# Starting places of the combinations and their weights in a Strassen-like MLP

## The chip, the cores and the metric

The kernel runs on one core of one Trainium2 chip. The metric is the device time of one execution in microseconds (us). The kernel before takes 1051.84 us (median of 3 runs, 1051.46 to 1052.83). A core has TensorE (matrix multiplication; a load of 128x128 weights and a matmul that streams a moving operand past them are two instructions, PEld and PE in the profile), VectorE (DVE), ScalarE (ACT), GpSimd (POOL) and the DMA queues that SyncE (SP) and POOL fill. SBUF is the working memory of 128 partitions, and a place in it is a byte address within a partition. PSUM takes TensorE's results.

## The reference

A decoder trunk of two layers over 512 tokens of width 1024, in float32. Layer 0 mixes by multi-head latent attention, layer 1 by gated linear attention; each mixer is followed by an MLP.

```python
x = x + mix
x = x + sq_relu_mlp(rms_norm(x, norm_mlp[i]), mlp_w_up[i], mlp_w_down[i])

def sq_relu_mlp(xn, w_up, w_down):          # 1024 -> 4096 -> 1024
    hid = jnp.square(jax.nn.relu(xn @ w_up))
    return hid @ w_down
```

The change lies in the two MLPs alone.

## The kernel before

**Precision.** Every float32 operand is split into a high part (rounded to the type float32r) and a low part (what is left). A product is three matmuls: high weights by high input, high by low, low by high. Weights come from HBM by DMA into `wraw` (1024 columns of 4 bytes per partition) or `comb`; `piece` then takes a buffer `wh` and a buffer `wl` and calls `split`: ACT rounds into `wh` (L104), DVE subtracts into `wl` (L107). Each of the two tags has four buffers of 1152 float32r elements, used in turn by the up products, the down products, and the mixers. The piece's 1024 elements lie at an offset within the 1152: 128 elements as a rule, 120 elements for the up products of the MLPs (`W_AT` and `W_AT_UP`). All these buffers begin 32 bytes past a multiple of 128, so a piece begins 32 + 512 bytes (32 past a multiple of 128) as a rule, and 32 + 480 (at a multiple of 128) for the up products.

**The MLP.** `mlp` cuts the hidden width of 4096 into eight blocks of 512. The first block's up product is made plainly (`up_first`). For the other seven, the up product is made by a scheme with seven products of half-sized blocks in place of eight, the down products likewise. `step` holds one block's sequence: seven `up_product`s for the next block and seven `down_product`s for this one, interleaved in an order written out by hand (`order`, `ends`). Four of the seven up products of a step have as input a linear combination of the input's quadrants, T1 to T4; three have a quadrant itself (`"11"`, `"21"`, `"22"`), which lies in the `set` tiles that the norm has written (hi and lo parts of 512 tokens, 32 bytes past a multiple of 128).

**The combinations.** `quadrants` runs once per MLP, before the first step. DVE and ACT make the four sums in the `comb` buffers 2 to 5 (L882 to L886), and `signed` splits each into a tile of its own, T2, T3, T1, T4: ACT writes the high parts (L837), DVE the low parts (L838). A tile holds 4 blocks of 128 features, each with 256 high and 256 low elements, 8192 bytes per partition. Ahead of the four tiles an unused tile of 120 elements, `gap`, sets their place: it begins 64 bytes past a multiple of 128, so the T tiles begin 32 past one. The pool that holds all this (`fast`) goes over room that the mixer has left; buffers `comb` 0 and 1 are taken after the T tiles.

**An up product** (L949) is 24 matmuls: two blocks of 128 hidden features, four blocks of 128 input features, three parts. Each loads 128x128 weights (512 bytes per partition from `wh` or `wl`) and streams 256 tokens (1024 bytes per partition from `set` or T). In the profile's names the T tiles appear as `T`, the quadrants as `set`:

```python
for n, (a_, x_) in enumerate(((wh, xh), (wh, xl), (wl, xh))):
    PE.matmul(o, a_, x_, ...)
```

**A down product** (L958) is 12 matmuls that load 128x128 of the hidden values and stream 512 columns of `wh` or `wl`.

The order of instructions on each engine is made by a list scheduler from the program's order and a cost model; waits follow from what each instruction reads and writes. While TensorE works at one product, ACT and DVE split the weights of the next ones, SP's queue loads raw weights, and POOL's queue adds second weight quadrants onto them (L928, L938).

Of the kernel before, what the change touches and what calls it, by code (L numbers as in the profile page):

```python
# [10 lines left out]
F32 = mybir.dt.float32  # L11
F32R = mybir.dt.float32r
# [6 lines left out]
P = 128  # L19
# [6 lines left out]
TH = S // 2  # L26
# [24 lines left out]
def trunk_kernel(ctx: ExitStack, tc: tile.TileContext, t_in: dict, out: bass.AP):  # L51
# [7 lines left out]
    def uname(s):  # L59
        count[0] += 1  # L60
        return f"{s}_{count[0]}"
# [40 lines left out]
    def split(src, hi, lo, hi_eng=ACT, lo_eng=DVE, order=lambda i: i):  # L102
        if hi_eng is ACT:
            order(ACT.activation(hi, src, AF.Copy))  # L104
        else:
            hi_eng.tensor_copy(hi, src)
        lo_eng.tensor_tensor(lo, src, f(hi), ALU.subtract)  # L107
# [26 lines left out]
        SP.dma_start(raw, src)  # L134
        return raw

    W_ROOM, W_AT, W_AT_UP = 1152, 128, 120

    def room_for(tag, a, n, at=W_AT):
        t = sb.tile([P, W_ROOM], F32R, tag=tag, bufs=4, name=uname(tag))  # L140
        return t[:, at : at + a * n].rearrange("p (a n) -> p a n", a=a)

    def piece(raw, a, n, order=lambda i: i, at=W_AT):
        hi = room_for("wh", a, n, at)
        lo = room_for("wl", a, n, at)
        split(raw, hi, lo, order=order)
        return hi, lo

    def cut(pair, *idx):
        return tuple(t[idx] for t in pair)  # L150
# [56 lines left out]
    def gcol(name, j):  # L207
        c = GAIN_COL[name] + j
        return gains[:, c : c + 1]
# [170 lines left out]
    def mla(layer, nrm, first, pools):  # L380
# [39 lines left out]
        for h in range(2):  # L420
            ks = slice(h * KH, (h + 1) * KH)
            SP.dma_start(raw[:, ks], w_in[:, :256].rearrange("(k p) n -> p k n", p=P)[:, ks])
            wq.append(piece(raw[:, ks], KH, 256))
# [12 lines left out]

        raw = col_chunk(w_in, 256, P)
        w = piece(raw, ND, P)
        p = bank("b")
        a_type(p, w, X)  # L440
# [33 lines left out]
        for k in range(2):  # L474
            SP.dma_start(raw[:, k], w_ukv[:, k, :, NOPE:])
        wv = [piece(raw[:, k : k + 1].rearrange("p a h c -> p a (h c)"), 1, D) for k in range(2)]
        V = [[None, None] for _ in range(NT)]
        VP = []
# [329 lines left out]
    def mlp(layer, nrm, nxt=None):  # L808
# [3 lines left out]
        KH = ND // 2  # L812
        first, second = slice(0, TH), slice(TH, S)
        es = ExitStack()
        fast = es.enter_context(tc.tile_pool(name=f"fast{layer}", bufs=1, reuse_waits="tile"))
# [11 lines left out]
        def comb(i):  # L827
            return fast.tile([P, 2 * S], F32, tag=f"comb{i}", bufs=1, name=uname("comb"))

        def by_k(t, n):  # L830
            return t.rearrange("p (k n) -> p k n", k=n)
# [4 lines left out]
        def signed(src, hi, lo, sign):  # L836
            ACT.activation(hi, src, AF.Copy, scale=sign)  # L837
            DVE.scalar_tensor_tensor(lo, src, sign, f(hi), ALU.mult, ALU.subtract)  # L838
# [34 lines left out]
        def quadrants():  # L873
            lead, trail = range(KH), range(KH, ND)
            quad["11"] = [nrm.parts[k][:, :, first] for k in lead]
            quad["21"] = [nrm.parts[k][:, :, first] for k in trail]
            quad["22"] = [nrm.parts[k][:, :, second] for k in trail]
            t1, t2, t3, t4 = (by_k(comb(i), KH) for i in range(2, 6))
            for k in lead:
                g1, g2 = (gcol(nrm.g, nrm.g0 + j) for j in (k, k + KH))  # L880
                u, v = xT[k], xT[k + KH]
                ACT.activation(t3[:, k], u[:, second], AF.Copy, scale=g1)  # L882
                DVE.scalar_tensor_tensor(t3[:, k], v[:, second], g2, t3[:, k], ALU.mult, ALU.subtract)
                DVE.scalar_tensor_tensor(t2[:, k], u[:, first], g1, t3[:, k], ALU.mult, ALU.add)
                DVE.scalar_tensor_tensor(t4[:, k], v[:, first], g2, t2[:, k], ALU.mult, ALU.subtract)
                DVE.scalar_tensor_tensor(t1[:, k], v[:, second], g2, t2[:, k], ALU.mult, ALU.subtract)  # L886
            fast.tile([P, 120], F32, tag="gap", name=uname("gap"))
            for name, t, sign in (("T2", t2, -1.0), ("T3", t3, 1.0), ("T1", t1, -1.0), ("T4", t4, -1.0)):
                parts = fast.tile([P, KH, 2, TH], F32R, tag=name, name=uname(name))
                signed(t, parts[:, :, 0], parts[:, :, 1], sign)  # L890
                quad[name] = [parts[:, k] for k in lead]

# [46 lines left out]
            return first_part  # L939

        def up_product(t, a, q, start):
            w = piece(a, KH, 256, at=W_AT_UP)
            for j in range(2):
                o = t[:, j * TH : (j + 1) * TH]
                for k in range(KH):
                    wh, wl = cut(w, slice(None), k, slice(j * P, (j + 1) * P))
                    xh, xl = quad[q][k][:, 0], quad[q][k][:, 1]
                    for n, (a_, x_) in enumerate(((wh, xh), (wh, xl), (wl, xh))):
                        PE.matmul(o, a_, x_, start=start and j == 0 and k == 0 and n == 0, stop=k == KH - 1 and n == 2, skip_group_check=True)  # L949
# [11 lines left out]
        def step(b, q, r, after):  # L961
# [24 lines left out]

            z = bank("u")
            up_product(z, a11, "11", True)
            y = bank("u")
            ACT.activation(y, z, AF.Copy)  # L990
# [5 lines left out]
            e = two_banks("e") if opening else begun(d)  # L996

            up_product(y, a12, "21", False)
            finish(y, 0, 0, r)
            DVE.tensor_tensor(a11, s1, a11, ALU.add)  # L1000
# [15 lines left out]
            def up_t2():  # L1016
                up_product(z, a11, "T2", False)
                u = part["u"] = tmp()
                ACT.activation(u, z, AF.Copy)
                DVE.tensor_tensor(a12, a11, a12, ALU.add)  # L1020
# [57 lines left out]

        up_first(Q[0])
        quadrants()  # L1080
        if not nxt:
            residual()
# [57 lines left out]
        q = Q[(NB - 1) % 2]  # L1140
        if nxt:
            room = [parts_room[(turn[0] + k) % 4] for k in range(4)]
# [5 lines left out]
            for c in range(2):  # L1148
# [10 lines left out]
                for j, p in enumerate(ps_):  # L1159
                    if j % 2 == 0:  # L1160
                        w = piece(last_raw[c][:, :, j * P : (j + 2) * P], 4, 256)
                    for k in range(4):
                        wh, wl = cut(w, slice(None), k, slice(j % 2 * P, (j % 2 + 1) * P))
# [525 lines left out]
    for k0, k1 in ((0, 1), (1, 2), (2, 4), (4, 6), (6, 8)):  # L1689
        w = piece(raw0[:, k0:k1], k1 - k0, KL, tc.keep_in_program_order)  # L1690
# [59 lines left out]
def build(nc, shapes):  # L1750
    args = {}
    for name, (shape, dt) in shapes.items():
        args[name] = nc.dram_tensor(f"in_{name}_dram", shape, dt, kind="ExternalInput").ap()
    o = nc.dram_tensor("out_0_dram", (S, D), F32, kind="ExternalOutput").ap()
    with tile.TileContext(nc) as tc:
        trunk_kernel(tc, args, o)
# [22 lines left out]
```

## Time and profile before

| | |
|---|---|
| median of 3 runs | 1051.84 us (1051.46 to 1052.83) |
| profiled execution | 1052.17 us, its span 1050.4 us |
| TensorE matmuls | 1040.9 us busy (99%), 5966 of them |
| TensorE weight loads | 909.7 us (87%) |
| VectorE, ScalarE, GpSimd | 874.3 us (83%), 699.3 us (67%), 113.9 us (11%) |
| L949, up products | 2352 matmuls: 1344 on T, 1008 on `set` |
| L958, down products | 1176 matmuls |

Matmuls overlap, so the mean duration of one is longer than the distance from start to start; where TensorE never idles, that distance, a step, is what the time is made of. A row of the chain or of the timeline with a count (x48) gives it as length divided by count. In the timeline a row of several gives the time from the first start to the last end. The two MLPs' steps run from about 206 to 476 us and from 747 to 1020 us of the span.

### The profile page before, as it was taken

Reading aid. Unit: us, or ns where it says so; the run is one execution under the profiler, and the core shown is the slowest. Engines: PE = TensorE matmul, PEld = TensorE weight load, DVE = VectorE, ACT = ScalarE, POOL = GpSimd, SP = SyncE. Lnnn points to the kernel's source line nnn. Section 1 sums busy time; section 2 is a strip of 40 time slices with the busy share of each in tenths; the row PEclk is TensorE's granted clock in tenths of the full one; section 3 lists DMA queues with packets and bytes.
Section 4 is the critical chain, followed back from the end, with each engine's and each line's share of the span. In section 5 each row is a group of like instructions: output and inputs, shape, how many; then the busy total and the mean of one; then the engine's idle time right before and its main releaser. Section 6 shows DMA issues by size and latency. Waiting matters only on the chain.

```text
span 1050.4 us, 15641 instructions
## 1 busy us (share of the span) xinstructions
PE 1040.9 (99%) x5966; PEld 909.7 (87%) x5966; DVE 874.3 (83%) x1340; ACT 699.3 (67%) x1074; POOL 113.9 (11%) x128
## 2 busy tenths in 40 slices
PE   9999999999999999999999999999999999999997
PEld 7788888899999999998888888888888999999995
DVE  7889977979889889888687399469889989989993
ACT  7667654677767777776445566555667777777784
POOL 7400010301011011000000000000010101111000
PEclk9999999999999999999999999999999999999999
DMA  7401235776876787843212222165496697687612
GB/s 232 121 21 41 81 96 145 230 194 153 225 201 155 190 221 163 194 160 121 68 64 80 87 75 75 48 162 159 89 249 160 164 240 178 153 232 187 155 61 81
DMA packets 120492, 149.97 MB, mean 143 GB/s; under 512 B 9344, under 2 KB 86144, under 8 KB 120288
## 3 DMA queue, kind: packets, MB, share of 16 engines
q1 hardware_dynamic: 95920, 117.76, 35.2%
q0 software_dynamic: 22400, 29.36, 17.4%
q10 hardware_dynamic: 2096, 1.84, 0.6%
q8 instruction: 47, 0.77, 0.3%
q14 instruction: 29, 0.24, 0.1%
HBM read 144.49 MB, written 4.19 MB: 142 GB/s over the span
## 4 chain that ended last, share of the span: by engine, by line
PE 93%; ACT 3%; DVE 2%; DMA 1%; issue 0%; ACTq 0%; SPq 0%; DVEq 0%
PE ps L949 26%; PE ps L958 26%; PE ps L112 10%; PE ps L114 10%; PE ps L113 10%; PE ps L1165 2%; PE ps L1420 1%; PE ps L129 1%; PE ps L1200 1%; PE ps L414 1%; PE ps L1547 1%; DVE wl L107 1%; PE ps L1470 0%; PE ps L677 0%; ACT wh L104 0%
## 5 line engine op out<-in xcount | busy, mean ns | idle before, releaser
L958 PE MATMUL ps<-wh,set 128*128 128x512 f32 x784 | 252.9, 391 | 0.1
L104 ACT ACTIVATE wh<-wraw 128x1024 fp32r<-128x1024 f32 x139 | 146.6, 1058 | 98.4 <-PE ps L113 39.4
L107 DVE TENSOR_TENSOR wl<-wraw,wh 128x1024 fp32r<-128x1024 f32 x139 | 169.7, 1221 | 46.1 <-ACT wh L104 45.2
L958 PEld LDWEIGHTS ps<-wh,set 128*128 128x128 f32 x784 | 147.0, 188 | 29.8 <-ACT set L104 0.5
L949 PE MATMUL ps<-T,wh 128*128 128x256 f32 x896 | 159.2, 279 | 0.0
L958 PE MATMUL ps<-wl,set 128*128 128x512 f32 x392 | 153.2, 391 | 0.0
L107 DVE TENSOR_TENSOR wl<-comb,wh 128x1024 fp32r<-128x1024 f32 x112 | 136.3, 1217 | 17.8 <-ACT wh L104 17.8
L949 PEld LDWEIGHTS ps<-T,wh 128*128 128x128 f32 x896 | 138.7, 188 | 2.7
L104 ACT ACTIVATE wh<-comb 128x1024 fp32r<-128x1024 f32 x112 | 118.0, 1054 | 25.5 <-PE ps L949 10.0
L949 PE MATMUL ps<-T,wl 128*128 128x256 f32 x448 | 125.0, 279 | 0.0
L949 PE MATMUL ps<-set,wh 128*128 128x256 f32 x672 | 119.7, 279 | 0.0
L112 PE MATMUL ps<-set,wh 128*128 128x512 f32 x280 | 109.5, 391 | 0.0
L113 PE MATMUL ps<-set,wh 128*128 128x512 f32 x280 | 109.4, 391 | 0.0
L114 PE MATMUL ps<-set,wl 128*128 128x512 f32 x280 | 109.1, 390 | 0.0
L949 PEld LDWEIGHTS ps<-set,wh 128*128 128x128 f32 x672 | 104.5, 188 | 2.6
L949 PE MATMUL ps<-set,wl 128*128 128x256 f32 x336 | 93.8, 279 | 0.0
L958 PEld LDWEIGHTS ps<-wl,set 128*128 128x128 f32 x392 | 73.6, 188 | 13.0
L949 PEld LDWEIGHTS ps<-T,wl 128*128 128x128 f32 x448 | 84.2, 188 | 0.1
L938 POOL DMA_DIRECT2D comb<-in_mlp_w_down_dram x28 | 33.8, 1207 | 302.0 <-DMA comb<-in_mlp_w_down_dram 112.8
L949 PEld LDWEIGHTS ps<-set,wl 128*128 128x128 f32 x336 | 63.2, 188 | 0.0
L113 PEld LDWEIGHTS ps<-set,wh 128*128 128x128 f32 x280 | 52.6, 188 | 10.8 <-DVE set L743 0.2
L114 PEld LDWEIGHTS ps<-set,wl 128*128 128x128 f32 x280 | 52.6, 188 | 10.8
(396 smaller groups left out, 2023.0 us busy)
## 6 DMA issues: line engine op xcount, KB each, us to landing
comb<-in_mlp_w_down_dram SPq DMA_DIRECT2D x74, 512.0 KB, 4.6
wraw<-in_mlp_w_up_dram SPq DMA_DIRECT2D x32, 1024.0 KB, 7.9
comb<-in_mlp_w_down_dram POOLq DMA_DIRECT2D x28, 512.0 KB, 7.5
wraw<-in_gla_w_in_dram SPq DMA_DIRECT2D x12, 1024.0 KB, 5.1
comb<-in_mlp_w_up_dram SPq DMA_DIRECT2D x14, 512.0 KB, 4.2
comb<-in_mlp_w_up_dram POOLq DMA_DIRECT2D x14, 512.0 KB, 8.6
wraw<-in_mlp_w_up_dram POOLq DMA_DIRECT2D x14, 512.0 KB, 6.1
wraw<-in_mla_w_o_dram SPq DMA_DIRECT2D x4, 1024.0 KB, 4.9
```

The costliest lines, as they stand in the source:

```text
L104: order(ACT.activation(hi, src, AF.Copy))
L107: lo_eng.tensor_tensor(lo, src, f(hi), ALU.subtract)
L112: PE.matmul(psum, wh, xh, start=start, stop=False)
L113: PE.matmul(psum, wh, xl, start=False, stop=False)
L114: PE.matmul(psum, wl, xh, start=False, stop=stop)
L129: PE.transpose(psum, src, ident[: src.shape[0], : src.shape[0]])
L414: PE.matmul(p, w[:, i, j * P : (j + 1) * P], x, start=start, stop=stop)
L938: POOL.dma_start(t, q(b, *more), accum_op=ALU.add)
L949: PE.matmul(o, a_, x_, start=start and j == 0 and k == 0 and n == 0, stop=k == KH - 1 and n == 2, skip_group_check=True)
L958: PE.matmul(o, x_, w_, start=start and k == 0 and n == 0, stop=k == 1 and n == 2, skip_group_check=True)
L1165: PE.matmul(p, a, x, start=False, stop=k == 3 and n == 2, skip_group_check=True)
L1200: PE.matmul(o, a, b_, start=False, stop=k == 3 and n == 2, skip_group_check=True)
```

## The change

The four T tiles become one tile, `room`, of 4 x 2048 + 4 elements, and the combinations lie in it from its fifth element on, one behind the other. The `gap` ahead of it has 96 elements in place of 120. The combinations so begin 80 bytes past a multiple of 128 where they began 32 past one. `piece` and `room_for` take an offset for `wh` and one for `wl`. The up products on quadrants keep 120 and 120; those on T take 124 for `wh` and 60 for `wl`. Since the buffers begin 32 past a multiple of 128 (and of 512), the T products' high weights begin 16 bytes past a multiple of 512 and the low weights 272 past one (both 16 past a multiple of 128). Nothing is added to the instructions or taken from them.

```diff
-    W_ROOM, W_AT, W_AT_UP = 1152, 128, 120
+    W_ROOM, W_AT = 1152, 128
+    AT_UP = {False: (120, 120), True: (124, 60)}
...
-    def piece(raw, a, n, order=lambda i: i, at=W_AT):
-        hi = room_for("wh", a, n, at)
-        lo = room_for("wl", a, n, at)
+    def piece(raw, a, n, order=lambda i: i, at=(W_AT, W_AT)):
+        hi = room_for("wh", a, n, at[0])
+        lo = room_for("wl", a, n, at[1])
         split(raw, hi, lo, order=order)
         return hi, lo
...
-            fast.tile([P, 120], F32, tag="gap", name=uname("gap"))
-            for name, t, sign in (("T2", t2, -1.0), ("T3", t3, 1.0), ("T1", t1, -1.0), ("T4", t4, -1.0)):
-                parts = fast.tile([P, KH, 2, TH], F32R, tag=name, name=uname(name))
+            fast.tile([P, 96], F32, tag="gap", name=uname("gap"))
+            size = KH * 2 * TH
+            room = fast.tile([P, 4 * size + 4], F32R, tag="T", name=uname("T"))
+            for i, (name, t, sign) in enumerate((("T2", t2, -1.0), ("T3", t3, 1.0), ("T1", t1, -1.0), ("T4", t4, -1.0))):
+                parts = room[:, 4 + i * size : 4 + (i + 1) * size].rearrange("p (k a t) -> p k a t", k=KH, a=2)
                 signed(t, parts[:, :, 0], parts[:, :, 1], sign)
                 quad[name] = [parts[:, k] for k in lead]
...
-            w = piece(a, KH, 256, at=W_AT_UP)
+            w = piece(a, KH, 256, at=AT_UP[q[0] == "T"])
```

## The prediction

> **What bounds the kernel now.** I read the page's busy times first, then the chain that ended last, then the chain and the timeline inside the two MLPs, where the changed products run.
>
> ```profile
> PE 1040.9 (99%) x5966; PEld 909.7 (87%) x5966; DVE 874.3 (83%) x1340; ACT 699.3 (67%) x1074; POOL 113.9 (11%) x128
> PEclk9999999999999999999999999999999999999999
> PE ps L949 26%; PE ps L958 26%; PE ps L112 10%; PE ps L114 10%; PE ps L113 10%; PE ps L1165 2%; PE ps L1420 1%; PE ps L129 1%; PE ps L1200 1%; PE ps L414 1%; PE ps L1547 1%; DVE wl L107 1%; PE ps L1470 0%; PE ps L677 0%; ACT wh L104 0%
> L949 PE MATMUL ps<-T,wh 128*128 128x256 f32 x896 | 159.2, 279 | 0.0
> L949 PE MATMUL ps<-T,wl 128*128 128x256 f32 x448 | 125.0, 279 | 0.0
> ```
>
> TensorE is busy 99% of the span at full clock, and the chain runs over its lines. The line of the up products, L949, holds 26% of the chain. The two T rows count the matmuls whose moving operand is one of the four combinations: 896 with wh and 448 with wl, 1344 together. Their idle time is 0.0, so no operand is ever late; what the change can move is the pace of the stream itself. That pace is not in the column of means (279 ns), because matmuls overlap; it is the distance between starts. The busy time by stage shows that this holds through both MLPs (columns: stretch, its length, then busy time and count of PE, PEld, DVE, ACT, POOL):
>
> ```profile
> 206.00:476.00 270.00, 269.97 (x1758) 246.21 (x1757) 238.96 (x265) 198.70 (x249) 32.25 (x27) 1.00 0.72 182
> 747.00:1020.00 273.00, 272.95 (x1784) 248.96 (x1783) 245.13 (x274) 202.45 (x255) 30.06 (x24) 1.00 0.69 173
> ```
>
> TensorE stands idle for 0.03 and 0.05 us there, and VectorE has 31 and 28 us to spare. Now the chain in order of time, around one step of an MLP (start, length, what, how many matmuls):
>
> ```profile
> 331.41 5.47 PE ps L958 x24
> 336.88 5.60 PE ps L949 x48
> ```
>
> The 48 matmuls from 336.88 are two T products of 24. 5.60 us / 48 = 116.7 ns from start to start, so one T product takes 2.80 us and all 56 of them (1344 / 24) take 156.8 us. The timeline inside such a product shows that the distance is not even:
>
> ```profile
> 300.52 0.28 PE L949 MATMUL ps<-T,wh 128*128 128x256 f32 x1
> 300.63 0.28 PE L949 MATMUL ps<-T,wl 128*128 128x256 f32 x1
> 300.75 0.40 PE L949 MATMUL ps<-T,wh 128*128 128x256 f32 x2
> 300.98 0.28 PE L949 MATMUL ps<-T,wl 128*128 128x256 f32 x1
> ...
> 302.38 0.28 PE L949 MATMUL ps<-T,wl 128*128 128x256 f32 x1
> 302.50 0.28 PE L949 MATMUL ps<-T,wh 128*128 128x256 f32 x1
> ```
>
> From 300.63 to 302.38 there are 15 steps in 1.75 us, again 116.7 ns, but the first step above is 0.11 us and the next one 0.12 us, with operands of the same shape. Something stretches some steps and not others.
>
> What stretches them? Two other streams give the floor and a comparison. A transpose streams only 128 columns, so its pace is set by the load of its 128x128 weights. The last row is a run of 256-column matmuls whose moving operand (S) begins at a multiple of 128 bytes and whose weights (qd) begin 64 past one:
>
> ```profile
> 478.02 1.91 PE L1158 MATMUL ps<-ident,xT 128*128 128x128 f32 x16
> L1158 PE MATMUL ps<-ident,xT x32: 272/273/273, 478.0 to 492.3; 128*128 128x128 f32 x32
> 601.01 1.22 PE L1547 MATMUL ps<-S,qd 128*128 128x256 f32 x9
> ```
>
> Sixteen transposes take 1.91 us with a last duration of 0.273, so a step is (1.91 - 0.273) / 15 = 109.1 ns: the load's own pace. The nine matmuls on S take (1.22 - 0.28) / 8 = 117.5 ns (0.28 is one matmul of this width, above). So a 256-column matmul is paced 7.6 ns above the load alone, and the two rows of that width differ by 0.8 ns.
>
> **The change part by part.** The profiled execution took 1052.17 us: its span is 1050.4, and 1.8 lies around it. It stands 0.33 above the median of 1051.84, which I take as the base for the final number.
>
> *One tile for four.* The first product could wait for all four combinations instead of its own. The writes that end the last combination, and the first product that reads one:
>
> ```profile
> 190.92 3.49 DVE L838 SCALAR_TENSOR_TENSOR T<-comb,T 128x1024 fp32r<-128x1024 f32 x3
> 214.54 0.40 PE L949 MATMUL ps<-T,wh 128*128 128x256 f32 x2
> 730.65 3.49 DVE L838 SCALAR_TENSOR_TENSOR T<-comb,T 128x1024 fp32r<-128x1024 f32 x3
> 758.30 0.40 PE L949 MATMUL ps<-T,wh 128*128 128x256 f32 x2
> ```
>
> All four are complete at 194.41 and 734.14; the first readers start 20.1 and 24.2 us later. Cost nothing; the cover is that distance. The one tile also needs its whole room free before its first write. The last tenant from the mixer before the second MLP is g, and the first write is this:
>
> ```profile
> 688.40 0.60 PE L129 MATMUL ps<-ident,g 128*128 128x128 f32 x4
> 726.13 1.04 ACT L837 ACTIVATE T<-comb 128x1024 fp32r<-128x1024 f32 x1
> ```
>
> g is done at 689.00, 37.1 us ahead. Nothing again.
>
> *The gap and two comb buffers.* The gap shrinks by 96 bytes and the room grows by 16, so the two comb buffers behind it move by 64 bytes (with rounding to 32). No instruction is added, and no queue (SP's and POOL's DMAs included) is passed by another. Nothing.
>
> *Writing the split weights 16 bytes past.* Of the 251 pieces of 1024 columns, 56 belong to T products. What rows there are for the same two operations at different starting places differ by 4 ns:
>
> ```profile
> L104 ACT ACTIVATE wh<-wraw 128x1024 fp32r<-128x1024 f32 x139 | 146.6, 1058 | 98.4 <-PE ps L113 39.4
> L104 ACT ACTIVATE wh<-comb 128x1024 fp32r<-128x1024 f32 x112 | 118.0, 1054 | 25.5 <-PE ps L949 10.0
> L107 DVE TENSOR_TENSOR wl<-wraw,wh 128x1024 fp32r<-128x1024 f32 x139 | 169.7, 1221 | 46.1 <-ACT wh L104 45.2
> L107 DVE TENSOR_TENSOR wl<-comb,wh 128x1024 fp32r<-128x1024 f32 x112 | 136.3, 1217 | 17.8 <-ACT wh L104 17.8
> ```
>
> 56 x 4 ns is 0.2 us of work that lies beside TensorE. It would have to be 1 us for each of the 28 pieces of one MLP before VectorE's 28 us of room were gone. Nothing on the path.
>
> *Reading them.* This is the whole price. Each T matmul streams its moving operand while the next weights are loaded. Today the moving operand begins 32 bytes past a multiple of 128 and the weights at one; afterwards 80 and 16 past. No TensorE operand of the kernel before begins 16 or 80 past, so the step is bounded. Below: 109.1 ns, the load alone, would save 1344 x 7.6 = 10.2 us. Above: every step at the 0.12 us that some steps already take costs 1344 x 3.3 = 4.4 us. The row with the same distance of 64 bytes between the operands (S and qd) is the nearest by placement: +0.8 ns, 1.1 us more, which is no measurable difference. The nearest by operands is the T stream itself, which already takes 0.11 us in part of its steps. I choose the latter: two streams whose starts lie further apart, with the low part of the weights 256 bytes away from the high part's phase (16 past 512, against 272 past it), should meet less regularly, and the long steps should go. I take a mean of 114.3 ns, between the 0.11 and the present 116.7. Sum: 1344 x (116.7 - 114.3) = 3.2 us less, 1048.9 for the profiled execution, 1048.6 from the median. With these steps shorter nothing else becomes late: wh and wl have four buffers each, and 3.2 us less over two MLPs leaves VectorE 1.6 us less room in each MLP, some 29 and 26 us.
>
> [...]
>
> [...]
>
> **The rivals.** *A placement makes no difference* (or none beyond 1.5 ns a step). For it: the row on S, at another placement, is within 0.8 ns of the T row, and the set products at L949 have the same mean (279 ns) as the T ones:
>
> ```profile
> L949 PE MATMUL ps<-set,wh 128*128 128x256 f32 x672 | 119.7, 279 | 0.0
> ```
>
> Against it: the uneven steps. It gives 1051.8, or 1052.9 with the 1.1 us of the S row. [...]
>
> *The new places meet more often*, on the other side: the load and the stream collide in every step instead of some, the step becomes 120 ns, and 1344 x 3.3 = 4.4 us make 1056.3. For it: the 0.12 us steps exist, and today's places give the shortest mean of the two rows of this width, so another place may well be worse. It decides from a mean of 118.3 ns upward (2.1 us / 1344 = 1.6 ns).
>
> *The load runs free*: the step falls to the floor and the time to 1041.6. For it is only that the transposes reach the floor; nothing shows a 256-column stream there. I count it inside the faster case, as its tail.
>
> **How the numbers follow.** A measurement of this kernel can tell about 0.2%, 2.1 us, from no change. Faster by more than that needs a mean step under 115.1 ns: 0.48, the forecast of 1048.6 and its tail to the floor (0.06 for under 112 ns). Within 0.2%: 115.1 to 118.3 ns, 0.27, where the S row lies. Slower: 0.25, around 1056.3, with some of it just over the limit. The faster case's own range is 1045.5 to 1049.7. To leave out 2 in 10, the range goes from 1045.8 (a step of 112.2 ns) to 1055.6 (119.5 ns): some 0.07 lie below and 0.12 above.
>
> **What the changed profile would show.** In the chain, two T products in a row (x48) should last 5.49 us instead of 5.60, and the timeline should show T steps of 0.11 us nearly throughout; set products should keep 2.80 us for 24 and down products 5.47 us for 24 (two products), and the idle time of L949 should stay 0.0. The L104 and L107 rows should keep their means within 1%. A T product of 2.80 us says that placement does nothing; 2.84 us or more says collisions. If the T products' time stays and the total moves, the cause is one of the parts that I priced at nothing: then the wait for T, or the idle time of TensorE ahead of L949, has grown. The prediction is wrong if the T steps become longer, since its sign rests on one choice that no row decides.

## The result, and the profile after

The changed kernel takes 1049.49 us (median of 10 runs, 1048.75 to 1049.67), the kernel before 1052.19 in the runs beside it (median of 10, 1051.46 to 1052.83). The ratio is 0.9975 with a 95% interval from 0.9965 to 0.9984: 2.7 us faster. The span of the profiled execution fell from 1050.4 to 1048.0. The lines have moved: up products are L952 now, down products L961.

On the changed kernel's page, the groups of the T stream:

```profile
L952 PE MATMUL ps<-T,wh 128*128 128x256 f32 x896 | 156.3, 276 | 0.0
...
L952 PE MATMUL ps<-T,wl 128*128 128x256 f32 x448 | 123.9, 277 | 0.0
```

Its busy time by stage (columns as before):

```profile
206.00:476.00 270.00, 269.92 (x1763) 245.98 (x1763) 240.21 (x267) 199.26 (x250) 32.32 (x27) 1.00 0.72 182
747.00:1020.00 273.00, 272.89 (x1783) 248.48 (x1783) 244.46 (x274) 202.56 (x255) 30.06 (x24) 1.00 0.68 173
```

TensorE still does not idle; what has changed is its pace. The chain of the changed kernel over one step of the MLP (start, length, what, count):

```profile
297.88 5.49 PE ps L952 x48
303.37 5.48 PE ps L961 x24
308.85 5.55 PE ps L952 x48
314.40 5.47 PE ps L961 x24
319.87 5.59 PE ps L952 x48
...
328.19 2.80 PE ps L952 x24
```

Before, every one of these groups of 48 was 5.60 us. The first (T2 and T1) is now 5.49, 114.4 ns a matmul; the second (a quadrant, then T3) 5.55; the third (T4, then quadrant 11 of the next block) only 5.59, though half of it is a T product. The quadrant product that stands alone keeps 2.80, and two down products 5.47. The timeline of the first group shows the shape of the gain:

```profile
297.72 0.40 PE L952 MATMUL ps<-T,wh 128*128 128x256 f32 x2
297.96 0.28 PE L952 MATMUL ps<-T,wl 128*128 128x256 f32 x1
298.08 0.40 PE L952 MATMUL ps<-T,wh 128*128 128x256 f32 x2
298.31 0.28 PE L952 MATMUL ps<-T,wl 128*128 128x256 f32 x1
298.43 0.40 PE L952 MATMUL ps<-T,wh 128*128 128x256 f32 x2
298.67 0.28 PE L952 MATMUL ps<-T,wl 128*128 128x256 f32 x1
...
300.03 0.28 PE L952 MATMUL ps<-T,wl 128*128 128x256 f32 x1
...
302.41 0.28 PE L952 MATMUL ps<-T,wl 128*128 128x256 f32 x1
```

From 297.96 to 298.67 six steps take 0.71 us, 118 ns each: no better than before. From 300.03 to 302.41 there are 21 steps in 2.38 us, 113.3 ns each, evenly. So the stream does not run faster from the start; it needs some eight steps here (five in T3) to fall into an even pattern, and then stays in it. Before, it never did: by the starts in the trace its steps go round in fours, 120, 113, 116 and 118 ns.

The quadrant product behind T4, with operands that the change leaves alone, lost:

```profile
322.71 0.28 PE L952 MATMUL ps<-set,wl 128*128 128x256 f32 x1
...
323.77 0.28 PE L952 MATMUL ps<-set,wl 128*128 128x256 f32 x1
```

Nine steps in 1.06 us are 117.8 ns, where the quadrant product that stands alone has 2.80 / 24 = 116.7. The same two places have two paces; the maps below show that what ran ahead decides between them.

By the starts in the two traces, all 1344 T matmuls together take 2.7 us less, the quadrant products 0.25 us more, and the down products 0.1 us less.

### The profile page after: what moved, and what is told of

Read it like the earlier page. It is cut to its first block, busy times and chain, and to the rows that moved or that the text cites. A ratio compares the mean times of both kernels' runs of the same rounds, so it can differ in the third digit from the quotient of the medians.

```text
span 1048.0 us, 15641 instructions
## 1 busy us (share of the span) xinstructions
PE 1039.6 (99%) x5966; PEld 908.3 (87%) x5966; DVE 873.9 (83%) x1340; ACT 699.1 (67%) x1074; POOL 114.5 (11%) x128
## 4 chain that ended last, share of the span: by engine, by line
PE 94%; ACT 3%; DVE 2%; issue 0%; ACTq 0%; DVEq 0%
PE ps L961 26%; PE ps L952 25%; PE ps L112 10%; PE ps L114 10%; PE ps L113 10%; PE ps L1168 2%; PE ps L1423 1%; PE ps L129 1%; PE ps L1203 1%; PE ps L415 1%; PE ps L1550 1%; DVE wl L107 1%; PE ps L1690 0%; PE ps L1473 0%; PE ps L678 0%; PE ps L674 0%
## 5 line engine op out<-in xcount | busy, mean ns | idle before, releaser
L961 PE MATMUL ps<-wh,set 128*128 128x512 f32 x784 | 253.2, 391 | 0.2
L104 ACT ACTIVATE wh<-wraw 128x1024 fp32r<-128x1024 f32 x139 | 146.6, 1058 | 97.4 <-PE ps L113 41.0
L107 DVE TENSOR_TENSOR wl<-wraw,wh 128x1024 fp32r<-128x1024 f32 x139 | 169.5, 1220 | 42.7 <-ACT wh L104 41.8
L961 PEld LDWEIGHTS ps<-wh,set 128*128 128x128 f32 x784 | 147.0, 188 | 29.8 <-ACT set L104 0.6
L952 PE MATMUL ps<-T,wh 128*128 128x256 f32 x896 | 156.3, 276 | 0.0
L961 PE MATMUL ps<-wl,set 128*128 128x512 f32 x392 | 152.9, 390 | 0.0
L107 DVE TENSOR_TENSOR wl<-comb,wh 128x1024 fp32r<-128x1024 f32 x112 | 136.3, 1217 | 17.5 <-ACT wh L104 17.5
L952 PEld LDWEIGHTS ps<-T,wh 128*128 128x128 f32 x896 | 137.6, 188 | 2.4
L104 ACT ACTIVATE wh<-comb 128x1024 fp32r<-128x1024 f32 x112 | 118.2, 1055 | 24.7 <-PE ps L952 9.5
L952 PE MATMUL ps<-T,wl 128*128 128x256 f32 x448 | 123.9, 277 | 0.0
L952 PE MATMUL ps<-set,wh 128*128 128x256 f32 x672 | 120.0, 280 | 0.0
L114 PE MATMUL ps<-set,wl 128*128 128x512 f32 x280 | 109.1, 390 | 0.0
L952 PEld LDWEIGHTS ps<-set,wh 128*128 128x128 f32 x672 | 104.7, 188 | 2.6
L952 PE MATMUL ps<-set,wl 128*128 128x256 f32 x336 | 93.9, 279 | 0.0
L961 PEld LDWEIGHTS ps<-wl,set 128*128 128x128 f32 x392 | 73.7, 188 | 13.2
L952 PEld LDWEIGHTS ps<-T,wl 128*128 128x128 f32 x448 | 84.1, 188 | 0.1
L952 PEld LDWEIGHTS ps<-set,wl 128*128 128x128 f32 x336 | 63.2, 188 | 0.0
```

What stands on the lines that cost most here:

```text
L114: PE.matmul(psum, wl, xh, start=False, stop=stop)
L961: PE.matmul(o, x_, w_, start=start and k == 0 and n == 0, stop=k == 1 and n == 2, skip_group_check=True)
```

## The experiments

A pair of places is written (weights, moving operand), in bytes modulo 256: the kernel before has (0, 32) in both the T and the quadrant products, the changed kernel (16, 208) in the T products. Times of kernels with one run are single values. The kernel before took 1052.28 us on the chip of the two halves and of the moved low weights, 1052.17 on that of the moved quadrants, the even places and the longer gap, and 1052.49 on that of the single tile and the last two timed kernels.

### Each half of the change alone

The first kernel keeps the combinations' place and undoes the weights':

```diff
-    AT_UP = {False: (120, 120), True: (124, 60)}
+    AT_UP = {False: (120, 120), True: (120, 120)}
```

> The combinations stay 80 bytes past a multiple of 128, the weights of their products go back to a multiple of 128 (120 and 120). Theory D (the distance between the start of the moving operand and that of the weights counts, 64 bytes of 128 is good; here it is 80): T products lose most of the gain, a mean step of 116 to 118 ns, a span 1.5 to 4 us above the 1048.0 of the changed kernel. Theory C (what counts is where the combinations begin, whatever the weights): the T steps stay at 113 to 115 ns, the span at 1048. Theory W (the weights' place alone counts): the T steps are those of before, 116.7 to 117, the span 1050.4.

The second keeps the weights' place and undoes the combinations':

```diff
-            fast.tile([P, 96], F32, tag="gap", name=uname("gap"))
+            fast.tile([P, 120], F32, tag="gap", name=uname("gap"))
...
-                parts = room[:, 4 + i * size : 4 + (i + 1) * size].rearrange("p (k a t) -> p k a t", k=KH, a=2)
+                parts = room[:, i * size : (i + 1) * size].rearrange("p (k a t) -> p k a t", k=KH, a=2)
```

> The combinations go back to 32 bytes past a multiple of 128 (still in one tile), the weights of their products stay 16 past (124 and 60). Distance 16. Theory D: no lock, T steps of 116 to 118 ns, span 1050 to 1052. Theory C: as before, 116.7 to 117 ns. Theory W: the T steps stay at 113 to 115 ns, span 1048.

1055.16 and 1053.85 us, spans of 1053.5 and 1052.1. In their chains the pair T2 and T1, the first kernel's row first:

```profile
298.21 5.72 PE ps L952 x48
```

```profile
298.78 5.63 PE ps L952 x48
```

119.2 and 117.3 ns a matmul, at the pairs (0, 208) and (16, 32). Each half alone is slower than the kernel before (116.7); only together do they gain. Theories C and W fall. Theory D foresaw both losses, but the first is larger than its range: 119.2 ns and a span 5.5 us above the changed kernel's. The first also comes near the 120 ns of the prediction's losing rival: at another place these matmuls take 119.2 ns, 2.5 more each than in the kernel before.

### One tile alone

The changed kernel with both places undone, only the single tile kept (the edits of both kernels above).

> One tile for the four combinations, but at the old place (32 bytes past a multiple of 128, gap of 120 elements) and with the old weights (120 and 120). All theories of placement: the kernel before, T steps of 116.9 ns with transitions, span 1050.4 within 0.5 us. If the single tile itself had brought or cost something (waits, order): a span off by more than 0.5 us.

1051.76 us, a span of 1050.1, and the same groups of 5.60 us as before. The tile itself does nothing, as priced.

### The low weights at the high weights' place

```diff
-    AT_UP = {False: (120, 120), True: (124, 60)}
+    AT_UP = {False: (120, 120), True: (124, 124)}
```

> As the changed kernel, but the low weights begin 16 bytes past a multiple of 512 like the high ones (124 and 124), not 272 past. Theory L (the 256 bytes between the low and the high weights' phase break up the regular collisions, as the prediction argued): T steps go back to 116 to 118 ns, span 1050 to 1052. Theory D (distance within 128 bytes alone): nothing changes, 113 to 115 ns in the T products and a span within 0.5 us of 1048.0.

1049.56 us, a span of 1047.8, and the pair T2 and T1 as in the changed kernel:

```profile
297.71 5.49 PE ps L952 x48
```

Theory L falls: the 256 bytes between low and high weights do nothing. They were part of the prediction's own reason.

### Maps of the places

The scan streams groups of matmuls of one pair of places and nothing else:

```python
for i in range(STEPS):
    n, k, j = i % 3, i // 3 % 4, i // 12 % 2
    at = (1152 + lo if n == 2 else 0) + wo + k * 256 + j * 128
    xt = xo + k * 512 + (256 if n == 1 else 0)
    keep(PE.matmul(a[:, :256], w[:, at : at + 128], x[:, xt : xt + 256], ...))
```

> A kernel that leaves out the whole computation: it streams 128 groups of 48 matmuls of 256 columns, as in two T products, each group at another placement, with six matmuls of 512 columns ahead of each group: moving operand 0 to 496 bytes past a multiple of 512 in steps of 16, high weights 0 or 16 past, low weights the same or 256 further. Theory D: the step depends on the distance between the moving operand and the weights modulo 128 and repeats four times over the 512 bytes, with about 113.3 ns at 64; the same at weights 0 and 16 if the moving operand is shifted along. Theory L: the groups with equal low and high weights never come under 116 ns and those with 256 between do. No effect of placement: all 128 groups within 0.5 ns.

Rows of its timeline: weights at 0 with the moving operand at 32 (the places before), then weights at 16 with the moving operand at 80 and at 208. A step is (length - 0.28) / 47.

```profile
25.27 5.83 PE L46 MATMUL a<-x,w 128*128 128x256 f32 x48
...
272.10 5.84 PE L46 MATMUL a<-x,w 128*128 128x256 f32 x48
...
328.85 5.62 PE L46 MATMUL a<-x,w 128*128 128x256 f32 x48
```

118.1, 118.3 and 113.6 ns; from start to start, which leaves out the end of the last matmul, the first is 117.8. The groups at 256 bytes further repeat theirs within 0.1 ns (the first, at the start of the run, apart), and so do those whose low weights lie 256 further: the pattern has a period of 256 bytes, not 128, so theory D as it was stated falls, and theory L falls again (with that period the low weights of the changed kernel lie at the same place as the high ones). Over the groups a step lies between 113.6 and 120.0 ns. One contradiction is open here: the pair before has 117.8 ns in the scan and 116.7 in the kernel. So all pairs modulo 256 were run, and the pair before behind different work.

> A kernel that leaves out the whole computation: groups of 30 matmuls of 256 columns at all 256 pairs of places modulo 256 in steps of 16 bytes (weights and moving operand), three matmuls of 512 columns ahead of each; then the pair of before (weights 0, moving 32) behind 1 to 6 matmuls of 512; then two pairs directly behind each other, 24 matmuls each. D256: in every row of weights the pair with the moving operand 192 further is near 113.3 ns in its last 15 steps. P: only some rows have it. On history (the same pair has 116.7 ns in the kernel before and 117.9 in the first scan): if the entry decides which pattern a pair falls into, the six groups and the pair behind another pair differ by 1 ns or more; if not, they are all alike.

The step in ns, worked out from the 256 groups as (length - 0.28) / 29 and rounded; rows are the weights' place, columns the moving operand's, in bytes modulo 256 (the first group holds the start of the run and is left out). Each pair was run once, behind three matmuls of 512 columns; from start to start the values are the same within 0.3 ns:

```
 w\mv    0   16   32   48   64   80   96  112  128  144  160  176  192  208  224  240
   0     -  119  117  118  118  118  120  114  119  119  118  119  118  119  118  117
  16   118  117  117  118  117  114  118  120  120  120  120  117  119  114  118  120
  32   118  117  120  119  117  118  118  118  120  115  120  119  119  119  118  119
  48   118  120  118  118  120  118  117  118  118  120  118  120  120  118  120  114
  64   118  119  118  118  120  119  117  118  118  120  119  115  118  119  117  119
  80   119  114  118  120  118  118  120  118  117  113  118  120  120  120  120  118
  96   119  119  114  119  118  117  120  117  117  119  118  118  120  115  119  118
 112   120  117  119  114  118  120  118  118  120  118  117  118  118  120  120  120
 128   119  119  117  119  118  119  118  117  119  119  117  118  118  120  120  113
 144   119  120  120  117  119  115  123  120  118  118  119  118  117  118  118  120
 160   120  115  119  119  117  119  114  119  118  117  120  119  117  118  118  120
 176   118  120  119  120  120  118  119  114  118  120  118  118  120  118  117  114
 192   118  118  120  115  118  119  119  119  118  119  118  117  120  119  117  118
 208   117  118  118  119  117  120  120  117  119  114  118  120  118  118  120  118
 224   117  118  118  118  120  115  118  119  117  119  114  119  118  117  120  119
 240   120  118  117  118  118  120  120  120  120  118  119  114  123  120  118  117
```

The median is 118.3 ns. Only 22 of the 256 pairs stand at 113 to 115: the moving operand 192 further than the weights in all eight rows whose weights begin at an odd multiple of 16, and in three even rows; 112 further in all eight even rows; 64 further in three odd ones. The changed kernel's pair (16, 208) is one of the first kind. D256 holds for all odd rows but only three even ones; P is nearer the truth.

On what ran ahead, from the same timeline: the pair before (weights 0, moving operand 32) behind one and behind two matmuls of 512 columns; then the pair (16, 208) and, directly behind it (L53), the pair before:

```profile
1095.51 3.69 PE L49 MATMUL a<-x,w 128*128 128x256 f32 x30
...
1099.51 3.66 PE L49 MATMUL a<-x,w 128*128 128x256 f32 x30
...
1129.54 2.92 PE L49 MATMUL a<-x,w 128*128 128x256 f32 x24
1132.30 2.99 PE L53 MATMUL a<-x,w 128*128 128x256 f32 x24
```

The step is 117.6 ns in the first, 116.6 in the second, and (2.99 - 0.28) / 23 = 117.8 behind the new pair; behind itself the pair keeps 116.7 from start to start. So one pair has more than one pattern, and what runs ahead chooses. That is the quadrant product behind T4: the pair (16, 208) ahead of it, and 117.8 ns there too. The number of matmuls ahead does not explain it alone: behind two, three, four, five and six matmuls of 512 columns the pair has the same step within 0.1 ns, while the scan, with six ahead, has 117.8. What in the entry decides stays open.

### The quadrants moved to a distance of 192 too

```diff
-    AT_UP = {False: (120, 120), True: (124, 60)}
+    AT_UP = {False: (16, 80), True: (124, 60)}
```

> The changed kernel with the weights of the products on quadrants moved as well: 16 and 80 elements, so that they begin 96 past a multiple of 256 and the quadrants (32 past one) begin 192 bytes ahead of them modulo 256, as the combinations (208) do of their weights (16). Theory D256 (moving operand 192 bytes past the weights modulo 256 is a lock at 113.3 ns wherever the weights begin): steps on set fall from 117.2 to 114 to 115 ns, 1008 x 2.5 = 2.5 us off, a span near 1045.5, the time near 1047. Theory P (each pair of places is a case of its own, as the scan's rows for weights at 0 and 16 differ at other distances): set steps of 116 to 120 ns, span 1047 to 1051.

1049.26 us, a ratio of 0.9972 (0.9962 to 0.9983), not to be told from the changed kernel. D256's 1047 is missed; P's range holds the span of 1048.2. The chain, with T2 and T1, quadrant 22 and T3, T4 and quadrant 11, and a quadrant product alone:

```profile
956.34 5.49 PE ps L952 x48
...
967.30 5.57 PE ps L952 x48
...
978.34 5.49 PE ps L952 x48
...
986.57 2.83 PE ps L952 x24
```

Behind a T product the quadrant product falls into the even pattern (5.49 where 5.59 was); behind a down product it does not, and is slower than at its old place (2.83 for 2.80). The gains and losses cancel. The pair (96, 32), which the map shows at 114, depends on the entry, and the kernel's usual entry is the wrong one. The run of the map has both cases among its last groups: this pair behind six matmuls of 512 columns, and directly behind (16, 208):

```profile
1143.43 2.99 PE L49 MATMUL a<-x,w 128*128 128x256 f32 x24
...
1153.14 2.89 PE L53 MATMUL a<-x,w 128*128 128x256 f32 x24
```

(2.99 - 0.28) / 23 = 117.8 and (2.89 - 0.28) / 23 = 113.5 ns, as in the kernel.

### The same distance at even places, and the combinations 128 bytes further

The first kernel puts the combinations at 192 and their weights at 0 modulo 256 (`room` from its first element, 120 and 120); the second lengthens the gap:

```diff
-            fast.tile([P, 96], F32, tag="gap", name=uname("gap"))
+            fast.tile([P, 128], F32, tag="gap", name=uname("gap"))
```

> Combinations at 192 past a multiple of 256, their weights at a multiple of 512 (120 and 120): the same distance of 192, both at multiples of 64. The scan gives 113.3 ns in the steady part for this pair. D256: as the changed kernel, T steps of 114 to 115.2 ns, span 1047.5 to 1048.5. If places 16 past a multiple of 32 were what counts: 117 to 118 ns and a span near 1051.

> The changed kernel with the gap 128 bytes longer: the combinations still begin 80 bytes past a multiple of 128, but 80 and not 208 past a multiple of 256; weights at 16. D256 and the scan (118.3 ns for this pair): T steps near 118.3 ns, 1344 x 3.4 = 4.6 us more, span near 1052.5. A period of 128 bytes, as the prediction's talk of 64 bytes supposed: no difference to the changed kernel, span 1048.

1048.67 and 1047.25 us, spans of 1046.9 and 1045.6, the first at the pair (0, 192), the second at (16, 80). The pair T2 and T1 of each:

```profile
297.64 5.46 PE ps L952 x48
```

```profile
297.24 5.44 PE ps L952 x48
```

The odd multiple of 16 is not needed: 113.8 ns at even places, a little better than was expected. And the kernel with the combinations at 80 modulo 256 missed both its expectations the good way: 5.44 / 48 = 113.3 ns a step, so even from the first matmul on. For both pairs the two maps disagree, and each is right once: (0, 192) has 113.8 ns in the scan and 118 in the map, (16, 80) 118.3 in the scan and 114 in the map. A pair's step in one map does not tell what it does behind other work; the kernel has to be run. Its down products gain too (227.1 ns a matmul between T products, from 228.2; worked out from the starts in the trace).

### The timing, and one more product

The kernel with the longer gap again, in several executions; and the same with the weights of quadrant 11 at the place that worked behind T4:

```diff
-            w = piece(a, KH, 256, at=AT_UP[q[0] == "T"])
+            w = piece(a, KH, 256, at=(16, 80) if q == "11" else AT_UP[q[0] == "T"])
```

> The run with the gap 128 bytes longer again, timed: if its span of 1045.6 was no chance, 1047.0 to 1047.8 in the median, 0.9955 of the kernel before, and about 2 us under the changed kernel.

> The combinations 80 past a multiple of 256 as in the run with the gap 128 bytes longer, and the weights of the products on quadrant 11 at 16 and 80 elements (96 past a multiple of 256), since such a product fell into the even pattern where it came directly behind a T product and not behind a down product. Theory H (which pattern a pair of places falls into depends on what ran ahead): the 10 of 14 such products that follow a T product take 113.5 to 114 ns a step, 0.7 us off; the other 4 lose 0.1; span 1044.9, time 1046.6. Against H: no change, 1045.5, or set steps of 118 and a longer span.

The longer gap: 1047.61 us, ratio 0.9952 (0.9939 to 0.9966). With quadrant 11 moved: 1047.09 us, ratio 0.9950 (0.9937 to 0.9962). Both are faster than the kernel before, and every time of both lies below the changed kernel's lowest (1048.75, not measured beside them); the interval of the first ratio just touches that of the changed kernel. The chain of the second:

```profile
336.49 5.44 PE ps L952 x48
...
347.39 5.53 PE ps L952 x48
...
358.37 5.46 PE ps L952 x48
...
366.58 2.80 PE ps L952 x24
```

T4 with quadrant 11 takes 5.46 us where the longer gap alone left 5.52: the quadrant product behind T4 has 114.0 ns a step by the starts, as theory H foresaw. Ten such groups are 0.6 us, which the trace shows and the times, with overlapping intervals, cannot.

### Other widths

The scan with weights at 16, all 16 places of the moving operand, and six widths.

> A kernel that leaves out the whole computation: groups of 30 matmuls of 128, 192, 256, 320, 384 and 512 columns, weights 16 past a multiple of 256, moving operand 0 to 240 past one in steps of 16, three matmuls of 512 ahead of each group. If the uneven steps come from the load of the next weights meeting the stream while neither has time to spare: at 256 columns a spread from 113 to 120 ns over the places, at 384 and 512 columns (the stream alone sets the step) a spread under 1% and at 128 (the load alone) under 2%. If the placement delays the stream itself: a spread of 6 ns or more at 384 and 512 columns too.

Rows of the timeline: the three matmuls of 512 columns behind the last 128-column group, the first group of 192 columns, the three matmuls of 512 behind it, and the second group of 192; then a fast and a slow place of 256 and a slow and a fast one of 512:

```profile
130.61 1.59 PE L39 MATMUL b<-v 128*128 128x512 f32 x3
132.00 5.22 PE L46 MATMUL a<-x,w 128*128 128x192 f32 x30
137.06 0.88 PE L39 MATMUL b<-v 128*128 128x512 f32 x3
137.78 3.49 PE L46 MATMUL a<-x,w 128*128 128x192 f32 x30
...
219.56 3.57 PE L46 MATMUL a<-x,w 128*128 128x256 f32 x30
...
232.19 3.76 PE L46 MATMUL a<-x,w 128*128 128x256 f32 x30
...
442.86 7.16 PE L46 MATMUL a<-x,w 128*128 128x512 f32 x30
...
458.17 6.98 PE L46 MATMUL a<-x,w 128*128 128x512 f32 x30
```

The groups of 128 columns can't be compared with the rest, and the forecast for them stays untested. By the starts in the trace they all settle at 213.3 ns a step, but so does the first group of 192, up to 135.6 us, and then it takes 111; and the matmuls of 512 columns ahead of each group go from 427 ns a step to some 230 (1.59 us for three, then 0.88). So until 135.6 us of this run a matmul of 512 columns took about twice the step that it had afterwards (427 against some 230 ns), and one of 192 too (213.3 against 111).

At 192 columns the places differ by less than half a nanosecond around 111.6 ns (the first group apart). At 256 they run from 113.3 to 120.1, at 320 from 144.4 to 146.7, at 384 from 173.3 to 177.8, and at 512 from 226.7 to 233.3, in the last 15 steps of each group. So a spread of 6.7 ns is there at 512 columns, where a step is twice as long as the 109 ns at which the weight loads of the transposes follow one another in the kernel before; at 384 it is 4.5 ns, less than the 6 that was forecast. The theory that load and stream must both be tight falls: the step moves with the placement even where, by that figure, the load has time to spare. Whether the load's reads take part is not shown, since every matmul of the maps has a load beside it. Why some pairs run evenly, and what lengthens the steps of the others, stays open.

## Why the prediction was right

- *Where and how much.* The step of the T stream was to fall from 116.7 to 114.3 ns on average, for 3.2 us. The T2 and T1 groups did what was named (5.49 us), single T products less, since they spend a fifth to a third of their 24 steps on falling into the pattern. Over all T matmuls the step fell by 2.0 ns, from 116.9 to 114.9, which is 2.7 us: the term was sized a little too large.
- *The floor.* 109.1 ns, the pace of the 128-column transposes, was never reached; 113.3 is the lowest steady step at this width in any run. That the load alone sets the 109.1 was the prediction's reading of the transposes, whose loads start 109 to 110 ns apart from the second on, as their matmuls do; no run has a load without a matmul.
- *The parts at nothing.* The tile costs nothing, as the kernel with one tile alone shows. Nor does the writing of the weights: the means of the four L104 and L107 rows move by 1 ns at most (1058, 1055, 1220 and 1217 in the changed kernel). The prediction's 4 ns were no measure of it, since its rows are told apart by what they read, not by where they write. No run moves the two `comb` buffers alone, but the steps of the matmuls already add up to the whole gain.
- *The set products* were to keep 2.80 us. Those that stand alone did; those behind T4 went from 116.5 to 117.8 ns a step and took back 0.3 us (ten products of 24), a cost that the prediction put at nothing.
- *The reason was wrong.* "Two streams whose starts lie further apart, with the low part 256 bytes away" is not what does it: the low part does not matter, and of the 32 pairs of the map that lie 64 apart modulo 128, 14 are fast and 18 as slow as others, so that distance does not decide. Nor are the steps less regular: they fall into a pattern that repeats evenly, 113.3 ns each from 300.03 to 302.41. The sign was a choice that no row of before decided, and it was said so; the map puts 22 of 256 pairs in the fast kind, so a place taken at random would most likely have lost. That the forecast of the sign came true was in good part luck. The other rival's longer steps are what most places show, though no run shows that streams meet there: 197 of the 255 values of the map are 118 ns or more, and the half change with weights at 0 took 1055.16.
- *Two rows that could not tell.* The quadrant products, whose equal mean was counted for "no difference", lie at the very pair (0, 32) of the T products. The row on S, taken as the nearest by placement, is the pair (64, 128): 64 apart like (16, 208) modulo 128, but not modulo 256, and 118 ns in the map.
- *No difference.* With a load beside every matmul the step moves by up to 7 ns with the places, from 113 to 120 ns in the map (two pairs lie higher still, at 123 ns). Nor are all multiples of 16 alike: with the weights at 16, the map has 119, 114 and 118 ns for the moving operand at 192, 208 and 224.

## What to carry to other kernels

In a stream of matmuls that never idles, look at the distance between starts, not at the mean duration (here 116.7 against 279 ns): steps of one shape that run from 113 to 120 ns, as here, can't all be set by the column count. In this case the places of the two operands modulo 256 bytes were worth some per cent of that stream (113 to 120 ns a step in the map), and they went together: change both, and expect most pairs to be no better (22 of 256 stood at 113 to 115). Judge a pair inside the kernel, behind the work that really runs ahead of it; a map shows which pairs to try, not which one will win.

## What was not expected of the hardware

- One pair of places has several stable patterns: (0, 32) has 116.7 or 117.8 ns from start to start, by what runs ahead of it, and (16, 80) has 113.3 in the kernel and 118.3 in the scan. In the changed kernel the even pattern, once reached, kept to 112 to 115 ns a step up to the last matmul of the T products; fast groups of the maps took 3.57 us for 30 matmuls and 5.62 for 48, 113.4 and 113.6 ns a step over their whole length.
- In the scan of the widths the places mattered at 512 columns (226.7 to 233.3 ns), and not at 192 (111.6).
- TensorE ran at about half pace for 128 us without standing idle. In the scan of the widths, whose first matmul starts at 7.67 us, 512-column matmuls between the 128-column groups took 427 ns a step (some 230 later), and the full pace came at 135.6 us, 3.6 us after the first matmul of 192 columns. In the two other maps, whose groups have 256 columns, the first group alone took longer than the rest (7.21 us for 48 matmuls where later ones took 5.6 to 5.9, and 5.31 for 30 where they took 3.6 to 3.8), so there it came, by an estimate from these lengths, some 5 us after the first matmul. What kept the pace low is not shown. So compare the groups of a map only where the matmuls of one shape between them keep their pace.
